# One layer of a pooling and mLSTM backbone on one core: the pooling input and its gate as seven-product pairs ahead of the attention, kept in DRAM

## The chip, the cores and the metric

The kernel runs on one core of a Trainium2 chip. The metric is device time in microseconds (us) of one execution; the time of a kernel is the median of its runs. The core has a matrix engine (TensorE, in the profile PE; its weight loads PEld), a vector engine (DVE), an activation engine (ACT), GpSimd (POOL), and a sync engine (SP) that issues most DMAs. Each engine works off its own instructions in a fixed order, and an instruction that waits holds up everything behind it on its engine.

## The reference

512 latent tokens (8 rows of 64) of width 1024 and 256 context tokens go through one layer. Cut to what the change touches:

```python
a_lat = _modulate(x, norm_mix, sh1, sc1)
p = split(a_lat @ w_in)      # pool input u, q, k, v, o, gate of pool, gate of mLSTM, 16 gate columns
...
# pooling mixer: 4 groups of 256 channels, windows 2, 4, 8, 16 on the 8 x 64 grid
mean = window_sum(window_sum(u_g, w, rows), w, cols) / count
pool_out = concat((mean - u_g) @ w_pool[g]) * scale
# mLSTM: 4 heads of 256, both directions, chunks of 128, starting from the context's state
m_out = rmsnorm(h) * gain * sigmoid(o)
y = sigmoid(p[5]) * pool_out + sigmoid(p[6]) * m_out
x = x + g1 * (y @ w_out)
x = x + g2 * swiglu(modulate(x))      # then a final rmsnorm
```

## The kernel before, in words

All operands of the big products are split into a high and a low part, and one block product is three matmuls: high by high, high by low, low by high (`mm3`, L180 to L186, so lines 184, 185 and 186 are the three matmuls of nearly every projection). Channels lie on the 128 partitions, tokens along the free dimension. `lat_tile(idx)` (L403) computes one tile of the input projection, 128 channels by 512 tokens: 24 matmuls of 512 columns, after a weight tile has come by DMA (`wr`), ACT has cast its high part (`wh`, L154) and DVE has subtracted for the low part (`wl`, L155). The 48 tiles are numbered: U0 = 0 to 7 the pool input u, Q0 8 to 15, K0 16 to 23, O0 24 to 31 (output gate), G5 32 to 39 (gate of the pool branch), G6 40 to 47 (gate of the mLSTM branch). Six of them, `FIRST`, are computed in the opening stage loop that also makes the modulated activations `aT`, in six PSUM banks.

Then come four heads. For each head h the code writes, in this order: the values; the attention, in two halves of the tokens (`scores`, then `apply`, whose matmuls are L779 to L781), with a tile of the mLSTM gates as filler between scores and apply of each half; the two pool tiles `pooled(2h)` and `pooled(2h+1)`; the transposes (`turn`, L807) of the second half; the two tanh tiles of the pool gate (G5); `pool_mix` (the product with w_pool); the gating and the sum (`finish`, L831 and L832, which sends y to DRAM, `yd`); and queries and keys of the next head. Behind each `apply`, DVE normalises the rows (L784 to L799) and takes one or two late adaLN products of 128x1024 (`late_mod`, L524).

`pooled(j)` (L438) first computes its u tile on PE with `lat_tile(U0 + j)`. Then GpSimd clears a padded buffer `pa` (L456), ACT copies u from PSUM into it (L457), DVE takes the window sums by doubling (L463 or L468 over rows, L473 over columns), multiplies with the reciprocal counts (L480), subtracts u (L481), and `tsplit` makes the high part on ACT (L173) and the low part on DVE (L174). Those two parts, `pm`, are what `pool_mix` waits for. `pa` has one buffer.

The FFN further on is computed by pairs: one gate tile and one up tile together form a 2 by 2 block of weights, and a Strassen-like scheme of seven block products replaces eight. A block product has 12 matmuls of 256 columns, so a pair takes 84 (`prepare`, `front`, `back`, `strassen`, from L997). Sums of weights are taken on DVE, the low parts of two of the blocks by a DMA of GpSimd that accumulates.

The order on PE, ACT and DVE is written out by hand inside a few stages; elsewhere the instructions are put in an order when the program is built, close to the order of the code, with later code moved forward where it is free.

Of the kernel before, what the change touches and what calls it, by code (L numbers as in the profile page):

```python
# [17 lines left out]
P = 128  # L18
# [18 lines left out]
FIRST = (24, 40, 25, 41, 8, 9)  # L37
# [12 lines left out]
def layer_kernel(ctx: ExitStack, tc, xT, cT, w0, w1, wv0, wv, wada_a, wada_b, par, crow, bg, wpool,  # L50
# [33 lines left out]
    open_pool("mix", ("m", "pm", "pa", "pb"), "right")  # L84
    open_pool("kqp", ("kq", "q"))
    open_pool("st", ("x", "cx", "ada", "row"))
# [35 lines left out]
    V.tensor_scalar(half_ps, parm[:, C_PS:C_PS + KT], 0.5, None, ALU.mult)  # L122
# [3 lines left out]
    x_sb = []  # L126
    for k in range(0, KT, 2):
        xx = tl("x", [P, 2 * T], F32, KT // 2)
        nc.sync.dma_start(xx, xT[:, k * T:(k + 2) * T])
        x_sb += [xx[:, :T], xx[:, T:]]  # L130
# [61 lines left out]

    class SumSq:
# [61 lines left out]
    rs_x = S("m")  # L255
# [44 lines left out]
    rs_c = S("m")  # L300
# [18 lines left out]
    w_first = []  # L319

# [45 lines left out]
    for k in range(KT):  # L366
# [18 lines left out]
        if k in (5, 6):  # L385
            ctx_quad(4 * (k - 5))
    manual.__exit__(None, None, None)
    wv_first += vload(wv0, DH + NG, 1)
    acc0 = dict(zip(FIRST, acc0))

# [47 lines left out]
    def pooled(j):  # L438

        w = (2, 4, 8, 16)[j // 2]  # L440
        acc = lat_tile(U0 + j)
# [11 lines left out]
        u3 = acc.rearrange("p (r c) -> p r c", r=R)  # L453
# [3 lines left out]
        nc.scalar.copy(A[:, rl:rl + R, lw:lw + W0], u3)  # L457
# [68 lines left out]

    crow_s = small([P, D], "crow_s", home="pa")
    close_pool("st")
    open_pool("att", ("vh", "vl", "Sp", "E", "gate"))
# [54 lines left out]
    def gates():  # L584
# [98 lines left out]
        yield dict(g=g, gx=gx, m0=m0, c1=c1, em=em, ws=ws, rd=rd, sa0=sa0)  # L683

# [160 lines left out]
    crow_setup()  # L845
    for h in range(H):
# [12 lines left out]
        rest = attention(h, q_, k_, v, gt, mgate((2, 3, 4, 6)[h]))  # L859
        if h == H - 1:  # L860
            close_pool("att")
            close_pool("kqp")
# [73 lines left out]

# [3 lines left out]

    def kt(q, k):
        return tuple(t[:, k * TC:(k + 1) * TC] for t in q)
# [48 lines left out]
    def ptiles(h, l, o=0):  # L994
        return [(h[:, o + i * P:o + (i + 1) * P], l[:, o + i * P:o + (i + 1) * P]) for i in range(4)]

    def prepare(j):  # L997

        a = tl("wr", [P, WMAX], F32, 3)[:, :D]
        b = tl("ur", [P, D], F32, 2)  # L1000
        nc.sync.dma_start(b, wffi[2 * j + 1])
        nc.sync.dma_start(a, wffi[2 * j])
        a11, a12, a21, a22 = a[:, :T], a[:, T:], b[:, :T], b[:, T:]
        p = {}

        def direct(nm, w, dram=None):
            h, l = S("oh", F32R), S("ol", F32R)
            nc.scalar.copy(h, w)
            if dram is None:
                V.tensor_sub(l, w, h.bitcast(F32))  # L1010
            else:
                nc.scalar.activation(l, w, AF.Copy, scale=-1.0)  # L1012
                nc.gpsimd.dma_start(l, dram, accum_op=ALU.add)  # L1013
            p[nm] = ptiles(h, l)

        def summed(names, o, h, l):
            split(sg[:, o:o + D], h, l)
            for e, nm in enumerate(names):
                p[nm] = ptiles(h, l, e * T)

        yield
        sg = tl("sg", [P, 2 * D], F32, 1, LINE)
        s1, s2, s3, s4 = (sg[:, i * T:(i + 1) * T] for i in range(4))
        direct("A11", a11)
        V.tensor_add(s1, a22, a21)
        V.tensor_add(s2, s1, a11)
        summed(("S1", "S2"), 0, wide("gh"), wide("gl"))
        yield
        direct("A12", a12, wffi[2 * j][:, T:])
        yield  # L1030
        V.tensor_add(s3, a11, a21)
        V.tensor_add(s4, s2, a12)
        yield
        summed(("S3", "S4"), D, *(tl(t, [P, WMAX], F32R, 2, LINE)[:, :D] for t in ("wh", "wl")))
        yield
        direct("A22", a22, wffi[2 * j + 1][:, T:])
        yield p

    def prepared(j):
        for p in prepare(j):  # L1040
            pass
        return p

    banks = []

    def front(j, p):

        n = j % 3
        x, w, z, y = (banks[i][:, :TC] for i in (n, 3, 4 + j % 2, 6 + j % 2))
# [317 lines left out]
```

## Time and profile before

| | |
|---|---|
| median of 3 runs | 889.85 us (888.89 to 889.96) |
| the profiled execution | 891.24 us |
| its span, first to last instruction | 889.5 us |
| outside the span | 1.74 us |
| PE busy | 877.4 us, 99% of the span |
| DVE, ACT, POOL busy | 614.8, 434.7, 66.0 us |
| bytes moved by DMA | 120.87 MB |

A matmul is put down as busy from its start to a modelled end, so rows of PE overlap, and its pace is read from start to start. In a row of the timeline the first number is the start, the second the duration, and the bracket at the end tells how long the engine was idle before it and what released it. In a row of the windows stand, after the length, busy time and count of PE, PEld, DVE, ACT and POOL, the granted TensorE clock, the DMA share and GB/s.

### The profile page before, as it was taken

Reading aid. Unit: us, or ns where it says so; the run is one execution under the profiler, and the core shown is the slowest. Engines: PE = TensorE matmul, PEld = TensorE weight load, DVE = VectorE, ACT = ScalarE, POOL = GpSimd, SP = SyncE. Lnnn points to the kernel's source line nnn. Section 1 sums busy time; section 2 is a strip of 40 time slices with the busy share of each in tenths; the row PEclk is TensorE's granted clock in tenths of the full one; section 3 lists DMA queues with packets and bytes.
Section 4 is the critical chain, followed back from the end, with each engine's and each line's share of the span. In section 5 each row is a group of like instructions: output and inputs, shape, how many; then the busy total and the mean of one; then the engine's idle time right before and its main releaser. Section 6 shows DMA issues by size and latency. Waiting matters only on the chain.

```text
span 889.5 us, 15027 instructions
## 1 busy us (share of the span) xinstructions
PE 877.4 (99%) x5913; PEld 799.9 (90%) x5913; DVE 614.8 (69%) x1187; ACT 434.7 (49%) x823; POOL 66.0 (7%) x93
## 2 busy tenths in 40 slices
PE   9999999999999999999999999999999999999996
PEld 8689798899888998889988899999889998899995
DVE  4678676868876787767886767884376753866644
ACT  3464363555345453344555446763156732656541
POOL 0000010010000100001000000110011100111000
PEclk9999999999999999999999999999999999999998
DMA  9853022435252632435343830474266643766402
GB/s 350 319 190 117 25 71 61 166 111 173 74 194 76 192 117 83 159 102 159 138 132 118 298 105 5 130 199 117 75 175 145 166 106 96 189 143 146 116 1 95
DMA packets 41445, 120.87 MB, mean 136 GB/s; under 512 B 4480, under 2 KB 8864, under 8 KB 40352
## 3 DMA queue, kind: packets, MB, share of 16 engines
q1 hardware_dynamic: 35904, 109.96, 38.2%
q0 software_dynamic: 5472, 9.96, 6.8%
q8 instruction: 46, 0.75, 0.3%
q14 instruction: 23, 0.19, 0.1%
HBM read 116.22 MB, written 3.69 MB: 135 GB/s over the span
## 4 chain that ended last, share of the span: by engine, by line
PE 91%; DVE 4%; ACT 2%; issue 2%; DMA 0%; DVEq 0%; POOLq 0%; POOL 0%; ACTq 0%
PE ps L184 20%; PE ps L186 20%; PE ps L185 20%; PE pat L334 3%; PE ps L565 3%; PE ps L566 3%; PE ps L567 3%; PE pat L781 2%; PE pat L185 2%; PE pat L184 2%; PE pat L779 2%; PE pat L186 2%; PE pat L780 2%; PE pat L140 1%; PE ps L334 1%
## 5 line engine op out<-in xcount | busy, mean ns | idle before, releaser
L184 PE MATMUL ps<-a,wh 128*128 128x512 f32 (+1 forms) x368 | 138.9, 378 | 0.0
L185 PE MATMUL ps<-a,wh 128*128 128x512 f32 (+1 forms) x368 | 138.5, 376 | 0.0
L186 PE MATMUL ps<-a,wl 128*128 128x512 f32 (+1 forms) x368 | 138.3, 376 | 0.0
L154 ACT CAST wh<-wr 128x1024 fp32r<-128x1024 f32 (+3 forms) x78 | 78.8, 1010 | 116.0 <-PE ps L185 89.3
L155 DVE TENSOR_TENSOR wl<-wr,wh 128x1024 fp32r<-128x1024 f32 (+3 forms) x78 | 91.8, 1177 | 44.3 <-ACT wh L154 43.0
L186 PEld LDWEIGHTS ps<-a,wl 128*128 128x128 f32 x368 | 69.3, 188 | 12.6
L184 PEld LDWEIGHTS ps<-a,wh 128*128 128x128 f32 x368 | 69.3, 188 | 12.2
L185 PEld LDWEIGHTS ps<-a,wh 128*128 128x128 f32 x368 | 69.3, 188 | 11.8
L186 PE MATMUL ps<-act,wl 128*128 128x512 f32 (+1 forms) x224 | 77.9, 348 | 0.7 <-DVE wl L155 0.7
L184 PE MATMUL ps<-act,wh 128*128 128x512 f32 (+1 forms) x224 | 77.8, 347 | 0.0
L185 PE MATMUL ps<-act,wh 128*128 128x512 f32 (+1 forms) x224 | 77.6, 347 | 0.0
L566 PE MATMUL ps<-wl,a 128*128 128x256 f32 (+1 forms) x192 | 54.4, 283 | 0.0
L567 PE MATMUL ps<-wh,a 128*128 128x256 f32 (+1 forms) x192 | 54.3, 283 | 0.0
L565 PE MATMUL ps<-wh,a 128*128 128x256 f32 (+1 forms) x192 | 54.3, 283 | 0.0
L1013 POOL DMA_DIRECT2D ol<-in_wffi x38 | 33.4, 887 | 255.7 <-ACT ol L1012 87.4
L184 PE MATMUL ps<-hp,gh 128*128 128x256 f32 x176 | 50.1, 285 | 1.0 <-ACT pat L1051 1.0
L1222 DVE SCALAR_TENSOR_TENSOR x<-ps,lb,x 128x512 f32<-128x512 f32 (+1 forms) x32 | 19.6, 617 | 45.2 <-PE ps L186 45.2
L184 PE MATMUL ps<-hp,oh 128*128 128x256 f32 x176 | 49.2, 280 | 0.1
L185 PE MATMUL ps<-hp,gh 128*128 128x256 f32 x176 | 49.1, 279 | 0.0
L186 PE MATMUL ps<-hp,gl 128*128 128x256 f32 x176 | 49.1, 279 | 0.0
L185 PE MATMUL ps<-hp,oh 128*128 128x256 f32 x176 | 49.0, 279 | 0.0
L186 PE MATMUL ps<-hp,ol 128*128 128x256 f32 x176 | 48.9, 278 | 0.0
(321 smaller groups left out, 2528.3 us busy)
## 6 DMA issues: line engine op xcount, KB each, us to landing
wr<-in_w SPq DMA_DIRECT2D x42, 512.0 KB, 3.5
pb<-in_wada_b SPq DMA_DIRECT2D x32, 512.0 KB, 3.6
wr<-in_wffi SPq DMA_DIRECT2D x25, 512.0 KB, 3.9
ur<-in_wffi SPq DMA_DIRECT2D x19, 512.0 KB, 4.0
ol<-in_wffi POOLq DMA_DIRECT2D x38, 256.0 KB, 5.0
ada<-in_wada_a SPq DMA_DIRECT2D x8, 1024.0 KB, 8.8
wr<-in_wffo SPq DMA_DIRECT2D x16, 448.0 KB, 3.9
wr<-in_wout SPq DMA_DIRECT2D x8, 512.0 KB, 3.7
```

The costliest lines, as they stand in the source:

```text
L154: nc.scalar.copy(wh, raw[:, :n])
L155: V.tensor_sub(wl, raw[:, :n], wh.bitcast(F32))
L184: nc.tensor.matmul(dst, wh, ah, start=first and i == 0, stop=False, skip_group_check=on)
L185: nc.tensor.matmul(dst, wh, al, start=False, stop=False, skip_group_check=on)
L186: nc.tensor.matmul(dst, wl, ah, start=False, stop=last and i == n - 1, skip_group_check=on)
L334: nc.tensor.matmul(acc0[i], w_first[k][i][w], aT[k][x], start=k + w + x == 0, stop=k == KT - 1 and w == 1)
L565: nc.tensor.matmul(acc[:, :n], ah, wh, start=kk == 0, stop=False)
L566: nc.tensor.matmul(acc[:, :n], ah, wl, start=False, stop=False)
L567: nc.tensor.matmul(acc[:, :n], al, wh, start=False, stop=kk == KT - 1)
L779: nc.tensor.matmul(o, sh_, vh[:, s, :], start=n == 0, stop=False)
L1013: nc.gpsimd.dma_start(l, dram, accum_op=ALU.add)
L1222: V.scalar_tensor_tensor(x1[j][:, c], acc[:, c], g2[:, j:j + 1], x1[j][:, c], ALU.mult, ALU.add)
```

## The change

- The 16 tiles of u and of the pool gate (U0 + j, G5 + j) are taken out of the heads. They are computed as eight pairs by the seven-product scheme, directly behind the values of head 0 and ahead of keys, queries and attention. The scheme's functions become a class `Seven` (with `prepare`, `front`, `back`, `run` unchanged in what they issue), from which the FFN's `Gated` and the new `Pool` derive.
- For the pair sums of the activations, `modulate` also writes the modulated activation in full precision over x, and DVE forms four sums and splits them into `hg` (operands N1, N2, T3, T4).
- u goes to DRAM (`ud`), the tanh of the pool gate too (`td`); the product of output gate and mLSTM gate of tiles 0 to 2 also (`gd`). They are read back by SP's DMAs in the heads. `pooled(j)` no longer has a tile product or an ACT copy: after GpSimd's clearing, a DMA brings u into `pa`.
- `FIRST` now holds the tiles 26 and 42 in place of the queries 8 and 9, which are now computed after keys(0). The attention's filler tiles start at 3 in place of 2 (`mgate(3 + h)`).
- Pools are opened in another order, `crow_setup` comes later, and two runs of 8 and 9 unused 256-column matmuls (`dense`) stand near the end.

The diff, cut to its core (`Seven` holds the former functions of the FFN):

```diff
-FIRST = (24, 40, 25, 41, 8, 9)
+FIRST = (24, 40, 25, 41, 26, 42)
...
         nc.scalar.activation(h, t1, AF.Identity, bias=shift)
+        nc.scalar.activation(src, t1, AF.Identity, bias=shift)
...
+    def sum_rest(i):
+        w11, w12, w21, w22 = quarters(i)
+        V.tensor_sub(w12, w22, w12)
+        V.scalar_tensor_tensor(w22, w11, -1.0, w22, ALU.mult, ALU.subtract)
+        V.scalar_tensor_tensor(w21, w22, -1.0, w21, ALU.mult, ALU.subtract)
...
     def pooled(j):
-        acc = lat_tile(U0 + j)
...
         nc.gpsimd.memset(A, 0.0)
-        nc.scalar.copy(A[:, rl:rl + R, lw:lw + W0], u3)
+        nc.sync.dma_start(A[:, rl:rl + R, lw:lw + W0], ud[j].rearrange("p (r c) -> p r c", r=R))
...
+    class Pool(Seven):
+        def first(self, s, z):
+            tanh_half(s[:, :TC], z)
...
+        def later(self, j, s, y, q):
+            tanh_half(s[:, TC:], y)
+            nc.sync.dma_start(td[j], s)
+
+        def done(self, j, s, x, q):
+            nc.scalar.copy(q[:, :TC], x)
+            nc.sync.dma_start(ud[j], q)
...
+    v = values(0, wv_first)
+    gen = gates()
+    next(gen)
...
+    sevens.run(0, KT)
...
     for h in range(H):
-        tg = None
         if h == 0:
-            mgate_all(0)
-            mgate_all(1)
-            q_ = queries(0)
-        v = values(h, None if h else wv_first)
-        if h == 0:
-            gen = gates()
-            next(gen)
             k_ = keys(0)
             gt = next(gen)
-            tg = [tanh_tile(G5 + e, "m") for e in range(2)]
-        rest = attention(h, q_, k_, v, gt, mgate((2, 3, 4, 6)[h]))
+            q_ = queries(0)
+        else:
+            v = values(h)
+        rest = attention(h, q_, k_, v, gt, mgate(3 + h))
...
         rest()
-        if h > 1:
-            mgate_all(2 * h + 1)
-        if tg is None and h < H - 1:
-            tg = [tanh_tile(G5 + 2 * h + e, "tmp") for e in range(2)]
+        if h == H - 1:
+            mgate_all(KT - 1)
         yb = pool_mix(h, pp)
-        if h == H - 1:
-            tg = [tanh_tile(G5 + 2 * h + e, "tmp") for e in range(2)]
+        tg = [td_tile(2 * h + e) for e in range(2)]
         for e in range(2):
+            gd_tile(2 * h + e)
             gated(yb[e], tg[e], yb[e])
...
+    dense(8)
     sd = st2.rstd_cols(HALF[1])
+    dense(9)
```

On PE, at the end of head 1's attention, this is the order before. `pat457` is the last `apply`, `ps462` and `ps475` are the two u tiles, `pat488` the transposes, `ps490` and `ps495` the two pool-gate tiles, `ps502` the first product of `pool_mix`, whose operand `pm_473` is the first pooled tile.

```order
L780 MATMUL pat457_2681<-vl_370_2084,Sp_442_2572 128x258
L781 MATMUL pat457_2681<-vh_369_2083,Sp_443_2573 128x258
L184 MATMUL ps462_2709<-a_36_226,wh_464_2712 128x512
...
L186 MATMUL ps475_2760<-a_123_599,wl_478_2764 128x512
L807 MATMUL pat488_2811<-ident_107,tmp_454_2654 128x128 [waits DVE_49,Activation_49]
L807 MATMUL pat488_2811<-ident_107,tmp_454_2654 128x128
L807 MATMUL pat488_2811<-ident_107,tmp_459_2695 128x128 [waits DVE_49]
L807 MATMUL pat488_2811<-ident_107,tmp_459_2695 128x128
L184 MATMUL ps490_2819<-a_36_226,wh_492_2822 128x512 [waits Activation_49]
...
L186 MATMUL ps495_2852<-a_123_599,wl_498_2856 128x512
L184 MATMUL ps502_2890<-pm_473_2756,wh_500_2886 128x512 [waits Activation_49]
```

Between the last `apply` and `pool_mix` stand 48 matmuls, the four transposes, and 48 matmuls more, all of 512 columns.

At the same place of the changed kernel `pat583` is the last `apply`, `pat606` the transposes, `ps610` the first product of `pool_mix` with the first pooled tile `pm_595` and its low part `pm_596`, and `ps617` the first tile of the next head's queries.

```order
L984 MATMUL pat583_3704<-vl_496_3107,Sp_568_3595 128x258
L985 MATMUL pat583_3704<-vh_495_3106,Sp_569_3596 128x258
L1011 MATMUL pat606_3772<-ident_110,tmp_580_3677 128x128 [waits DVE_49,Activation_49]
L1011 MATMUL pat606_3772<-ident_110,tmp_580_3677 128x128
L1011 MATMUL pat606_3772<-ident_110,tmp_585_3718 128x128 [waits DVE_49]
L1011 MATMUL pat606_3772<-ident_110,tmp_585_3718 128x128
L186 MATMUL ps610_3785<-pm_595_3748,wh_608_3781 128x512 [waits Activation_49]
L187 MATMUL ps610_3785<-pm_596_3749,wh_608_3781 128x512 [waits DVE_49]
L188 MATMUL ps610_3785<-pm_595_3748,wl_609_3782 128x512
...
L186 MATMUL ps617_3817<-a_38_231,wh_619_3820 128x512
```

The 96 matmuls are gone from here: the transposes follow directly on `apply`, `pool_mix` on the transposes, and the queries stand behind the first six matmuls of `pool_mix`, of which the first two wait for ACT and for DVE.

On DVE, at the end of head 1, these rows lead to the first pooled tile before: the last normalisation of the second half, the two late products (`crow_s`), and the window sums from `pa_466` to the low part `pm_474`.

```order
L799 TENSOR_SCALAR tmp_459_2695<-tmp_459_2695,rst_384_2269 128x256 [waits DVE_49]
L524 SCALAR_TENSOR_TENSOR pb_460_2703,mods_145<-pb_460_2703,crow_s_695 128x1024 [waits DMAHW1_49]
L524 SCALAR_TENSOR_TENSOR pb_461_2706,mods_145<-pb_461_2706,crow_s_695 128x1024 [waits DMAHW2_49]
L155 TENSOR_TENSOR wl_493_2823<-wr_491_2820,wh_492_2822 128x1024 [waits DMAHW7_49,PE_49,Activation_49]
L463 TENSOR_TENSOR pb_467_2743<-pa_466_2740 128x670 [waits DVE_49,Activation_49]
L463 TENSOR_TENSOR pb_468_2745<-pb_467_2743 128x536 [waits DVE_49]
L473 TENSOR_TENSOR pb_469_2747<-pb_468_2745 128x528 [waits DVE_49]
L473 TENSOR_TENSOR pb_470_2749<-pb_469_2747 128x512 [waits DVE_49]
L480 TENSOR_TENSOR tmp_472_2753<-pb_470_2749,tmp_471_2751 128x512 [waits DMAHW4_49,DVE_49]
L481 TENSOR_TENSOR tmp_472_2753<-tmp_472_2753,pa_466_2740 128x512 [waits DVE_49]
L155 TENSOR_TENSOR wl_498_2856<-wr_496_2853,wh_497_2855 128x1024 [waits DMAHW0_49,PE_49,Activation_49]
L174 TENSOR_TENSOR pm_474_2757<-tmp_472_2753,pm_473_2756 128x512 [waits Activation_49]
```

Between them stand the low parts of two weight tiles (L155).

In the changed kernel the same stretch of DVE reads so; L1003 is the former L799, L682 the former L524, L621 to L639 the window sums, L1035 the former L831.

```order
L1003 TENSOR_SCALAR tmp_585_3718<-tmp_585_3718,rst_510_3292 128x256 [waits DVE_49]
L682 SCALAR_TENSOR_TENSOR pb_586_3726,mods_148<-pb_586_3726,crow_s_2002 128x1024 [waits DMAHW1_49]
L682 SCALAR_TENSOR_TENSOR pb_587_3729,mods_148<-pb_587_3729,crow_s_2002 128x1024 [waits DMAHW2_49]
L621 TENSOR_TENSOR pb_589_3735<-pa_588_3732 128x670 [waits DVE_49]
L1035 TENSOR_TENSOR m_616_3807<-m_616_3807,m_511_3293 128x512 [waits DMAHW4_49,Activation_49]
L621 TENSOR_TENSOR pb_590_3737<-pb_589_3735 128x536 [waits DVE_49]
L1035 TENSOR_TENSOR m_374_2452<-m_374_2452,m_512_3294 128x512 [waits Activation_49]
L631 TENSOR_TENSOR pb_591_3739<-pb_590_3737 128x528 [waits DVE_49]
L631 TENSOR_TENSOR pb_592_3741<-pb_591_3739 128x512 [waits DVE_49]
L638 TENSOR_TENSOR tmp_594_3745<-pb_592_3741,tmp_593_3743 128x512 [waits DMAHW5_49,DVE_49]
L639 TENSOR_TENSOR tmp_594_3745<-tmp_594_3745,pa_588_3732 128x512 [waits DVE_49]
L176 TENSOR_TENSOR pm_596_3749<-tmp_594_3745,pm_595_3748 128x512 [waits Activation_49]
```

The sums on `pa_588` still stand behind the last normalisation and the two late products. The two weight tiles have left the stretch, and the two products of `finish` (L1035) have moved into it.

More of the change, by code (lines that the diff above doesn't have):

```diff
@@ L1080, in strassen, with first, begin, later @@
[L1080 to L1103 removed]
+    class Gated(Seven):
+        def first(self, s, z):
+            nc.scalar.activation(s[:, :TC], z, AF.Silu)
+        def begin(self, j):
+            act_tiles(j)
+        def later(self, j, s, y, q):
+            nc.scalar.activation(s[:, TC:], y, AF.Silu)
+            V.scalar_tensor_tensor(s[:, TC:], q[:, TC:], -1.0, s[:, TC:], ALU.mult, ALU.mult)
+        def done(self, j, s, x, q):
+            V.scalar_tensor_tensor(s[:, :TC], x, -1.0, s[:, :TC], ALU.mult, ALU.mult)
+            split(s, *act[j])
@@ L1209, in layer_kernel @@
     st2 = SumSq((T // 2,))
-    banks += [PS() for _ in range(4)] + [PS("pat") for _ in range(4)]
+    banks[:] = [PS() for _ in range(4)] + [PS("pat") for _ in range(4)]
     turn_ = [0]
@@ L1248, in gain, with dense @@
         nc.scalar.activation(gained[i][j][:, 0, :], x1[j][:, HALF[i]], AF.Copy, scale=pcol(C_NFIN, j))
+    def dense(n):
+        for _ in range(n):
+            nc.tensor.matmul(banks[3][:, :TC], B11[0][:, :P], B11[0][:, :TC], start=True, stop=True)
     def final(i, sd, cuts):
```

290 lines of the change are left out of this document (175 added, 115 removed).

## The prediction

> **What bounds the kernel now.** I read the page first, for the busy shares and the PE row of the slices.
>
> ```profile
> PE 877.4 (99%) x5913; PEld 799.9 (90%) x5913; DVE 614.8 (69%) x1187; ACT 434.7 (49%) x823; POOL 66.0 (7%) x93
> PE   9999999999999999999999999999999999999996
> PEclk9999999999999999999999999999999999999998
> ```
>
> PE is busy from the first slice to the last, at full clock. So the time is the sum of PE's work, and everything else is hidden as long as PE has something to do. The windows then give the pace of the two kinds of work that are exchanged, and of head 1 (from 185.60 to 288.10), whose last part begins at the end of its attention.
>
> ```profile
> 143.91:165.74 21.83, 21.83 (x99) 17.98 (x97) 16.01 (x28) 7.68 (x14) 2.21 (x6) 1.00 0.40 133
> 587.57:597.47 9.90, 9.90 (x87) 9.90 (x86) 7.42 (x13) 6.63 (x12) 1.74 (x2) 1.00 0.68 165
> 185.60:288.10 102.50, 102.45 (x633) 92.14 (x632) 76.84 (x149) 47.49 (x94) 7.21 (x11) 1.00 0.42 131
> 235.50:288.10 52.60, 52.60 (x258) 44.47 (x257) 37.97 (x59) 22.35 (x37) 4.09 (x8) 1.00 0.35 115
> ```
>
> The first row is four projection tiles in a stretch (96 matmuls of 512 columns and three that overlap), 5.46 us a tile and 0.227 us a matmul. The second is one FFN pair of 84 matmuls, 9.90 us. In the third DVE is busy 77 of 102.5 us: there is slack, but it comes from PE's having so much to do.
>
> Then I read how PE passes the end of an attention. The timeline of PE at that place of head 1:
>
> ```profile
> 235.41 0.28 PE L781 MATMUL pat<-vh,Sp 128*128 128x258 f32 x1
> 235.53 0.40 PE L184 MATMUL ps<-a,wh 128*128 128x512 f32 x1
> ```
>
> PE goes on at 235.53 without a pause, because the next thing in its order is a u tile that depends on nothing. I call 235.53 zero. The timelines of DVE, ACT and GpSimd show what has to happen after it before `pool_mix` can start:
>
> ```profile
> 236.11 0.17 DVE L786 RECIPROCAL rec<-rec 128x1 f32<-128x1 f32 x1
> 238.91 0.62 DVE L799 TENSOR_SCALAR tmp<-tmp,rst 128x256 f32<-128x256 f32 x2 [0.81 <-POOL rst L797]
> 239.44 1.22 DVE L524 SCALAR_TENSOR_TENSOR pb<-pb,crow_s 128x1024 f32<-128x1024 f32 x1
> 241.73 0.09 DVE L524 DVE_READ_ACCUMULATOR pb<-pb,crow_s 128x1 f32 x1
> 243.22 0.85 DVE L463 TENSOR_TENSOR pb<-pa 128x670 f32<-128x670 f32 x1
> 244.11 0.72 DVE L463 TENSOR_TENSOR pb<-pb 128x536 f32<-128x536 f32 x1
> 244.86 1.43 DVE L473 TENSOR_TENSOR pb<-pb 128x528 f32<-128x528 f32 x2
> 247.05 0.69 DVE L481 TENSOR_TENSOR tmp<-tmp,pa 128x512 f32<-128x512 f32 x1
> 248.80 0.69 DVE L174 TENSOR_TENSOR pm<-tmp,pm 128x512 fp32r<-128x512 f32 x1
> 250.17 0.69 DVE L831 TENSOR_TENSOR m<-m,m 128x512 f32<-128x512 f32 x1
> ...
> 247.78 0.63 ACT L173 CAST pm<-tmp 128x512 fp32r<-128x512 f32 x1
> 247.89 0.72 POOL L456 MEMSET pa<- 128x737 f32 x1 [9.02 <-ACT m L809]
> ```
>
> The rows are normalised at +4.0, the late products end at +6.3, the six steps of the window sums take 243.22 to 247.74 = 4.5, the high part comes 0.7 later. All of that is hidden today: 96 matmuls, 21.8 us, lie between `apply` and `pool_mix`.
>
> **The change part by part.**
>
> *The products.* Removed are 16 tiles of 5.46 = 87.3 us of PE; added are eight pairs of 9.90 = 79.2. The balance is **-8.1 us**. All of it counts, since PE is the bound. If the pairs are not dense, the gain goes: in the pair of the profile DVE is busy 7.42 of 9.90 us and the DMA 0.68 of its share, so I bound this between 0 and +8 for the eight (1 us a pair), and take 0.
>
> *The ends of the four heads.* The orders above show that the 96 matmuls leave just the place where they cover the chain, and nothing takes it: `apply`, transposes, `pool_mix`. DVE's rows stay behind the last normalisation and the late products, though u itself lies ready in DRAM. For head 1, from zero:
>
> - The transposes run at +4.0, for 0.3.
> - The window sums begin at +6.3 instead of +7.7 (the weight subtraction between them, 1.23, is gone). With two `finish` products among them at 0.6 each from start to start (250.17 and its kind), they end at 6.3 + 4.5 + 1.2 = 12.0. The high part is ready at 12.6, the low part at 13.2. PE has idled 12.6 - 0.3 = 12.3, and 0.4 more for the low part.
> - Six matmuls but one, then 23 of the queries, 28 x 0.227 = 6.4: PE is at 19.6. The second pooled tile needs `pa`, which has one buffer: GpSimd clears it after 12.0 (0.72, at +12.8), and SP brings u. The nearest DMA rows are those of the same size:
>
> ```profile
> tmp<-in_icnt SPq DMA_DIRECT2D x2, 256.0 KB, 3.5
> yd<-tmp SPq DMA_DIRECT2D x2, 256.0 KB, 3.6
> ```
>
> With 3.5 it lands at 16.3; 4.5 of sums and 0.63 of cast make 21.4. PE waits 1.8, and 0.4 for the low part. SP holds no weight of the next projection behind that DMA; those for queries and keys were issued ahead of it.
> - The next query tile can't have its weight buffer cast until `pool_mix` is done with it:
>
> ```profile
> L154 ACT CAST wh<-wr 128x1024 fp32r<-128x1024 f32 x60 | 62.8, 1047 | 86.5 <-PE ps L185 68.1 <-issue 7.4 <-PE pat L185 5.4
> L155 DVE TENSOR_TENSOR wl<-wr,wh 128x1024 fp32r<-128x1024 f32 x60 | 73.4, 1223 | 39.9 <-ACT wh L154 38.7
> ```
>
> that is 1.05 for the cast and most of the 1.22 for the low part, less two matmuls, 1.9.
>
> Head 1 together: 12.3 + 0.4 + 1.8 + 0.4 + 1.9 = **16.8 us**.
>
> Head 2 has the same order on PE, with a longer chain (window 8):
>
> ```profile
> 345.68 1.19 DVE L463 TENSOR_TENSOR pb<-pa 128x994 f32<-128x994 f32 x1
> ...
> 350.18 1.22 DVE L155 TENSOR_TENSOR wl<-wr,wh 128x1024 fp32r<-128x1024 f32 x1
> 351.32 0.68 DVE L473 TENSOR_TENSOR pb<-pb 128x512 f32<-128x512 f32 x1
> ...
> 353.24 0.69 DVE L481 TENSOR_TENSOR tmp<-tmp,pa 128x512 f32<-128x512 f32 x1
> ```
>
> That is 8.25, with a weight subtraction (1.14 from start to start) and a `finish` product (0.6) among it: 6.5 of its own against 4.5. The first wait is 2.0 longer; the second too, less 0.1 that two more matmuls and a longer clearing make, 1.9; and there the rest of a tile covers the weights' 1.9. Together 16.8 + 2.0 + 1.9 - 1.9 = 18.8, **19 us**.
>
> Head 0 keeps cover: the two query tiles of head 1 (`q1`) stand between its `apply` and the transposes, 48 x 0.227 = 10.9. Its window of 2 has two sums fewer (1.4), so the first tile is ready in time. Its sums end at 6.3 + 3.1 + 0.6 (the low part of a small weight) = 10.0. The second comes at 10.0 + 0.8 (clearing) + 3.5 (DMA) + 3.1 (sums) + 1.2 (`finish` products) + 0.6 (cast) = 19.2. PE is at 10.9 + 0.3 + six matmuls = 12.6: **7 us** with the low part.
>
> Head 3 has its y splits on DVE among the sums. Before, normalisation and the two pooled tiles stand like this:
>
> ```profile
> 454.71 0.61 DVE L799 TENSOR_SCALAR tmp<-tmp,rst 128x256 f32<-128x256 f32 x2 [0.81 <-POOL rst L797]
> 467.24 0.69 DVE L174 TENSOR_TENSOR pm<-tmp,pm 128x512 fp32r<-128x512 f32 x1
> 473.01 0.69 DVE L174 TENSOR_TENSOR pm<-tmp,pm 128x512 fp32r<-128x512 f32 x1 [0.69 <-ACT pm L173]
> ```
>
> The first pooled tile is complete 12.6 after the normalisation, so at about +16.6. PE has there 13 matmuls, the transposes and 35 matmuls, some 12 us. I take 1 for the transposes, 4 for the first tile, 3 for the second (it now waits for clearing and DMA, 4.2, with 5 us of cover) and 2 for the weights of w_out: **10 us**, between 3 and 15.
>
> Sum of the heads: 16.8 + 19 + 7 + 10 = **+53**. If only the first waits of heads 1 and 2 came true it would be 12.3 + 14.3 = 27.
>
> *The stage and the hand-overs.* The sums for `hg` are pushed into DVE ahead of the low weights of the values, and that subtraction is barely in time today; keys(0) needs weights whose buffers the pairs have just left; in head 0 the filler tile of the attention is spent early on by the queries. The trace of before shows none of these waits. The nearest prices are one subtraction, 1.2, for each of the first two, and between nothing and one tile, 5.46, for the third. I take 1 + 1 + 3 = **+5** (0 to 8). The x written back by ACT in the stage is one activation more there, where ACT has room (49% over the span): 0. The 17 unused matmuls near the end stand where PE is waiting for the final norm: +0.2 at most.
>
> *The clock.* Idle stretches of 12 us are new for this kernel. What it shows of them lies at its two ends:
>
> ```profile
> 0.00:4.00 4.00, 2.64 (x12) 2.64 (x13) 1.10 (x10) 1.50 (x2) 0.94 (x6) 1.00 0.38 96
> 8.00:12.00 4.00, 4.00 (x39) 4.00 (x38) 3.58 (x6) 2.17 (x4) 0.00 (x0) 1.00 1.03 410
> 884.00:886.00 2.00, 0.00 (x0) 0.00 (x0) 1.24 (x3) 0.00 (x0) 0.00 (x0) 0.61 0.53 190
> ```
>
> The granted clock falls to 0.61 within a few us of the last matmul, and the first matmuls run at 0.22 us each where 8 us later they take 0.10. By these rows a restart costs up to some 3 us (about 8 us at a mean pace near 0.6). Most of it falls into a stretch that ends with another wait of PE, where it is covered. I take +1.5 in all, 0 to 11. [...]
>
> **The sum.** Against the profiled execution: 891.2 - 8.1 + 53 + 5 + 0.2 + 1.5 = 942.8. The median of before is 1.4 lower than its profiled run, so 941.4; I say **940**.
>
> **The rivals.**
>
> 1. *The chain is not in the way, and only the products count: faster.* For it, u is ready in DRAM hundreds of us before it is used, and the window sums need nothing of `apply`. If DVE reached them before the attention's last rows, PE's wait at a head's end would be only the 3.7 to the transposes less what cover there is; with queries moved forward into it too, heads cost nearly nothing: 891.2 - 8.1 + 2 - 1.4 = 884. It decides where the head ends cost under 8 us in all, 2 a head. Against it, DVE's order has the sums behind L1003 and L682. Chance 0.10.
> 2. *The waits are there, but only the first of heads 1 and 2:* 891.2 - 8.1 + 27 - 1.4 = 909, with the hand-overs 914. For it, my second waits rest on a DMA time and on small differences. Chance 0.15.
> 3. *The clock and the pairs add:* five restarts not covered, 11, and pairs 1 us longer, 8: 940 + 17 = 957. The DMA share of 0.68 speaks for some of it; against it, the FFN's pairs with the same share run densely. Chance 0.10. [...]
> 4. *The change does not alter the time:* the gain of 8.1 equals the waits. Nothing points to just that sum. Chance 0.02.
>
> My forecast has 0.63. 0.2%, 1.8 us, is about what a measurement of this kernel can tell from no change. Faster by more than that: rival 1, 0.10. Within it: rival 4 and what lies around it, 0.03. Slower 0.87. The range runs from 908, the low end of rival 2, to 956, near rival 3; it leaves out the faster case and a little at the top.
>
> **What would show it.** In the trace after: PE idle of 12 us in head 1 and 14 in head 2 ahead of the first product of `pool_mix`, released by ACT's `pm`; two to seven us before the second pooled tile in each head, with the DMA into `pa` landing late; a pair of 9.9 us; heads 20 us shorter in PE work and only some 5 us shorter in time. The prediction is wrong if PE is dense at the head ends, if DVE's sums stand ahead of the last `apply`, or if the pairs take clearly over 10 us.

## The result and the profile after

The changed kernel takes 940.05 us (median of 4 runs, 939.0 to 940.82), the kernel before, run beside it, 889.9. The ratio is 1.0555 [1.0538, 1.0573]: 50 us slower. The profiled execution took 939.8 us, its span is 938.0, and the mean granted clock of TensorE 0.973.

The page after, busy times and two rows of the slices:

```profile
PE 887.0 (95%) x6218; PEld 813.7 (87%) x6218; DVE 652.0 (70%) x1259; ACT 468.7 (50%) x903; POOL 80.5 (9%) x109
PE   9999999999799599958999699999999999999997
PEclk9999999999899799978999899999999999999999
```

Where before every slice of PE but the last showed a 9, there are now four dents, in slices 11, 14, 18 to 19 and 23, and the clock has them at the same places. They are the ends of the four heads. PE is busy 9.6 us longer although it has less to do, mostly because matmuls at half clock (granted 0.50) take longer. The waits of PE, in total, times and longest, say for what it waits:

```profile
PE ps L186 <- ACT pm L175: 27.7, 5, 9.7
PE pat L1011 <- DVE tmp L1003: 8.2, 3, 3.7
PE ps L186 <- ACT wh L156: 2.7, 2, 1.8
PE ps L720 <- DVE wl L157: 1.2, 1, 1.2
```

`pool_mix` waits for the high part of a pooled tile, and the transposes wait for the normalised rows. Both stand right behind the attention now. The timeline of PE at the end of head 1, the place that the prediction worked through:

```profile
314.38 0.28 PE L985 MATMUL pat<-vh,Sp 128*128 128x258 f32 x1
318.37 1.09 PE L1011 MATMUL pat<-ident,tmp 128*128 128x128 f32 x4 [3.71 <-DVE tmp L1003]
326.87 0.79 PE L186 MATMUL ps<-pm,wh 128*128 128x512 f32 x1 [7.41 <-ACT pm L175]
327.60 0.79 PE L187 MATMUL ps<-pm,wh 128*128 128x512 f32 x1
...
330.74 0.40 PE L188 MATMUL ps<-a,wl 128*128 128x512 f32 x1
...
335.62 0.74 PE L186 MATMUL ps<-pm,wh 128*128 128x512 f32 x2
```

Zero, counted as in the prediction, is 314.50. The transposes run at +3.9 (predicted 4.0) and the first product of `pool_mix` at +12.4 (12.6). Here is the chain that releases it, the timeline of DVE and then GpSimd's clearing:

```profile
317.87 0.62 DVE L1003 TENSOR_SCALAR tmp<-tmp,rst 128x256 f32<-128x256 f32 x2 [0.81 <-POOL rst L1001]
318.40 1.22 DVE L682 SCALAR_TENSOR_TENSOR pb<-pb,crow_s 128x1024 f32<-128x1024 f32 x1
...
320.69 0.85 DVE L621 TENSOR_TENSOR pb<-pa 128x670 f32<-128x670 f32 x1
321.46 0.69 DVE L1035 TENSOR_TENSOR m<-m,m 128x512 f32<-128x512 f32 x1
...
326.85 0.69 DVE L176 TENSOR_TENSOR pm<-tmp,pm 128x512 fp32r<-128x512 f32 x1 [0.68 <-ACT pm L175]
330.38 0.86 DVE L621 TENSOR_TENSOR pb<-pa 128x670 f32<-128x670 f32 x1 [2.84 <-DMA pa<-ud]
...
326.29 0.71 POOL L614 MEMSET pa<- 128x737 f32 x1 [8.45 <-DVE tmp L639]
```

Normalisation, two late products, six steps of sums with two `finish` products among them, then the second pooled tile behind clearing and DMA: the rows and their order are those of the forecast. The second tile is complete at +21.1 (predicted 21.4), but PE itself comes there only at 335.62, +21.1, and so does not wait.

The stretches, first of before and then of after: the end of each head, from the end of its `apply` to the same place in the next stage.

```profile
143.91:168.95 25.04, 25.04 (x115) 20.67 (x113) 18.81 (x31) 10.13 (x18) 2.21 (x6) 1.00 0.35 116
235.53:271.43 35.90, 35.90 (x163) 29.68 (x161) 26.20 (x40) 13.55 (x22) 2.66 (x6) 1.00 0.42 139
337.98:384.75 46.77, 46.77 (x211) 38.68 (x210) 33.67 (x48) 16.60 (x26) 2.57 (x6) 1.00 0.39 124
451.32:508.99 57.67, 57.67 (x258) 47.71 (x257) 40.85 (x71) 28.17 (x45) 1.33 (x2) 1.00 0.55 179
```

```profile
81.79:160.25 78.46, 78.38 (x675) 78.18 (x674) 48.72 (x84) 46.12 (x89) 12.80 (x15) 1.00 0.74 193
226.14:247.17 21.03, 15.91 (x66) 12.45 (x65) 15.91 (x29) 6.78 (x13) 2.20 (x6) 0.88 0.44 131
314.50:343.20 28.70, 17.52 (x67) 13.02 (x65) 20.14 (x34) 7.61 (x14) 2.65 (x6) 0.76 0.36 109
409.81:442.40 32.59, 18.29 (x66) 13.48 (x65) 22.92 (x35) 7.00 (x13) 2.57 (x6) 0.74 0.26 82
509.00:558.20 49.20, 41.13 (x162) 31.96 (x161) 33.98 (x66) 20.77 (x36) 1.32 (x2) 0.90 0.51 168
```

The first row of after is the eight pairs. In the others the heads lose 48, 96, 144 and 96 matmuls of 0.2275 us (two of the counts hold one more that overlaps the edge), that is 10.9, 21.8, 32.8 and 21.8 us, but get shorter by only 4.0, 7.2, 14.2 and 8.5. The remainder is what the head ends cost. The whole account, from the places of the same instructions in the two traces:

| stretch | predicted | measured |
|---|---|---|
| eight pairs in place of 16 tiles | -8.1 | 78.46 - 16 x 5.46 = -8.9 |
| stage and hand-overs | +5 (1 + 1 + 3) | 0.4 + 1.4 + 1.3 + 0.7 = +3.8 |
| end of head 0 | 7 | 6.9 |
| end of head 1 | 16.8 | 14.6 |
| end of head 2 | 19 | 18.6 |
| end of head 3 | 10 | 13.4 |
| clock outside these; rest | +1.5; +0.2 | +0.75; -0.6 |
| sum (heads predicted as 53) | +51.6 | +48.6 |

Of the 53.5 us of the four head ends, PE idles 38.7: that is length less PE busy in the rows above. Some 12 more, an estimate from the starts of PE's timeline, are lost by matmuls, nearly all of 512 columns, that start 0.43 us apart instead of 0.2275, at a granted clock of 0.50: 1.8, 2.7, 3.4 and 4.2 us in heads 0 to 3.

### The profile page after: what moved, and what is told of

It is laid out like the page before. It is cut to its first block, busy times and chain, and to the rows that moved or that the text cites. A ratio compares the mean times of both kernels' runs of the same rounds, so it can differ in the third digit from the quotient of the medians.

```text
span 938.0 us, 15999 instructions
## 1 busy us (share of the span) xinstructions
PE 887.0 (95%) x6218; PEld 813.7 (87%) x6218; DVE 652.0 (70%) x1259; ACT 468.7 (50%) x903; POOL 80.5 (9%) x109
## 5 line engine op out<-in xcount | busy, mean ns | idle before, releaser
L157 DVE TENSOR_TENSOR wl<-wr,wh 128x1024 fp32r<-128x1024 f32 (+3 forms) x62 | 72.4, 1169 | 30.3 <-ACT wh L156 29.2
L186 PE MATMUL ps<-a,wh 128*128 128x512 f32 (+1 forms) x240 | 90.0, 375 | 0.9 <-ACT wh L156 0.9
L187 PE MATMUL ps<-a,wh 128*128 128x512 f32 (+1 forms) x240 | 89.8, 374 | 0.0
L188 PE MATMUL ps<-a,wl 128*128 128x512 f32 (+1 forms) x240 | 89.4, 372 | 0.1
L175 ACT CAST wh<-sg 128x1024 fp32r<-128x1024 f32 x27 | 28.4, 1051 | 57.7 <-PE pat L187 47.7
L176 DVE TENSOR_TENSOR wl<-sg,wh 128x1024 fp32r<-128x1024 f32 x27 | 33.1, 1225 | 33.9 <-ACT wh L175 33.8
L186 PEld LDWEIGHTS ps<-a,wh 128*128 128x128 f32 x240 | 46.2, 192 | 8.9 <-ACT wh L156 1.3
L188 PEld LDWEIGHTS ps<-a,wl 128*128 128x128 f32 x240 | 46.0, 192 | 8.2 <-DVE wl L157 0.8
L187 PEld LDWEIGHTS ps<-a,wh 128*128 128x128 f32 x240 | 46.1, 192 | 7.1
L186 PE MATMUL ps<-hp,gh 128*128 128x256 f32 x176 | 50.2, 285 | 1.0 <-ACT pat L270 1.0
L186 PEld LDWEIGHTS ps<-act,wh 128*128 128x128 f32 x224 | 42.9, 191 | 8.0 <-ACT wh L156 2.5
L186 PE MATMUL ps<-hp,oh 128*128 128x256 f32 x176 | 49.2, 279 | 0.1
```

What stands on the lines that cost most here:

```text
L157: V.tensor_sub(wl, raw[:, :n], wh.bitcast(F32))
L175: nc.scalar.copy(h, src)
L176: V.tensor_sub(l, src, h.bitcast(F32))
L186: nc.tensor.matmul(dst, wh, ah, start=first and i == 0, stop=False, skip_group_check=on)
L187: nc.tensor.matmul(dst, wh, al, start=False, stop=False, skip_group_check=on)
L188: nc.tensor.matmul(dst, wl, ah, start=False, stop=last and i == n - 1, skip_group_check=on)
```

## The experiments

My theory: PE idles at the head ends because one chain on DVE (normalisation, late products, window sums, then clearing, DMA and sums again) lost the matmuls that covered it. Rivals: the loss lies in the clock, in the pairs, or in the DMA; or each cure only moves the wait. Every kernel below is the changed kernel with the edit shown. Medians are compared with the kernel before, timed beside it on the same chip (892.05, 890.4, 891.06 and 891.07 us for the four groups), and the differences are against that. The changed kernel itself was +50.2 with the result above and +50.7 in the second group.

**The changed kernel again**, as the yardstick of its group.

> The changed kernel once more, unaltered, as the measure for the two small edits beside it: 940 to 943.

Measured: 941.08 us, 1.0574 [1.056, 1.0589], +50.7. Its trace also shows what slow matmuls cost where no wait follows. In head 3, behind PE's last wait, the same 20 matmuls take 6.42 us in the first trace and 4.68 here, because the clock was back earlier. The windows, of the first trace and then of this one:

```profile
538.64:545.06 6.42, 6.42 (x21) 5.13 (x21) 6.34 (x9) 2.37 (x4) 0.00 (x0) 0.71 0.65 201
539.17:543.85 4.68, 4.68 (x20) 3.86 (x21) 4.59 (x7) 1.22 (x2) 0.00 (x0) 1.00 0.52 150
```

This trace comes to the stretch 0.5 us later than the first, and its span ends 1.3 us earlier (936.7 against 938.0). So here, as far as two traces can show it, the clock is paid in the time.

**Are the pairs worth what they cost?** The 16 tiles are computed at the new place, but as plain tiles.

```diff
-    banks[:] = [PS() for _ in range(4)] + [PS("pat") for _ in range(4)]
-    sevens.run(0, KT)
+    for j in range(KT):
+        s, q = S("tmp"), S("tmp")
+        tanh_half(s, lat_tile(G5 + j))
+        nc.sync.dma_start(td[j], s)
+        nc.scalar.activation(q, lat_tile(U0 + j), AF.Copy, scale=-1.0)
+        nc.sync.dma_start(ud[j], q)
```

> The seven products undone, the place kept: the 16 tiles of u and pool gate are computed ahead of the attention as plain tiles of 24 matmuls of 512 columns, stored to DRAM as before (the sums of activations for the pairs are still made). Theory: pairs took 78.5 us in the trace of the changed kernel, 16 tiles take 87.3, so 940 + 9 = 949, and the head ends wait as they do. Rival (the pairs gain nothing, their work is hidden or paid elsewhere): 940.

Measured: 951.55, 1.067 [1.0643, 1.0696], +59.5. The stage of the 16 tiles in its windows:

```profile
81.71:169.48 87.77, 87.35 (x387) 71.99 (x385) 26.54 (x39) 26.75 (x38) 0.00 (x0) 1.00 0.51 166
```

It is 87.8 us against 78.5, a difference of 9.3, and the time differs by 9. The waits of the head ends stay as they were (28.8 us for `pm` and 8.1 for the transposes, against 27.7 and 8.2). So the products give their gain in full, and the loss is all elsewhere.

**Is it the clock?** Unused matmuls keep PE at work in the two waits of heads 1 and 2.

```diff
...
+        if h in (1, 2):
+            warm(28)
         rest()
+        if h in (1, 2):
+            warm(54)
```

> The clock by itself: at the ends of heads 1 and 2, 28 unused matmuls of 256 columns (3.3 us) go between the last apply and the transposes and 54 (6.3 us) between the transposes and the first product of pool_mix, that is into time in which PE waits; their results are read by nothing. Theory: the half clock behind the two long waits (9 and 13 matmuls at 0.43 instead of 0.23 us in the trace of the changed kernel, some 2 and 3 us) is hidden, since the second pooled tile is ready only when PE arrives there; the time falls by under 1 us. Rival (each restart of the clock costs what its slow matmuls lose): 5 us less, 936.

Measured: 941.28, 1.057 [1.0551, 1.0588], +50.9: no difference from the changed kernel in the same group. The windows show that the cure took:

```profile
317.00:325.00 8.00, 7.33 (x60) 6.90 (x58) 7.85 (x14) 0.84 (x2) 0.01 (x1) 1.00 0.00 0
327.00:330.00 3.00, 3.00 (x15) 2.46 (x14) 0.00 (x0) 0.00 (x0) 0.00 (x0) 1.00 0.43 93
336.00:338.00 2.00, 2.00 (x5) 1.51 (x6) 0.87 (x2) 0.00 (x0) 0.23 (x1) 0.50 1.00 371
```

The clock is 1.00 through the wait and behind it, where the changed kernel has 0.50:

```profile
328.00:330.00 2.00, 2.00 (x6) 1.52 (x6) 0.00 (x0) 0.00 (x0) 0.00 (x0) 0.50 0.58 131
```

And the timeline of PE shows where the time went instead:

```profile
334.07 0.50 PE L186 MATMUL ps<-a,wh 128*128 128x512 f32 x1 [0.91 <-ACT wh L156]
335.84 1.09 PE L186 MATMUL ps<-pm,wh 128*128 128x512 f32 x2 [1.03 <-ACT pm L175]
```

A PE that keeps its pace arrives early at the second pooled tile and at the next weights, and waits there; a new slow stretch of some 3.4 us begins at 336 (the clock is 0.51, 0.50, 0.50 and 0.78 in the four us from there, 1.00 behind them). From the end of `apply` to the keys, head 1 takes 30.28 us against 28.70 in the changed kernel, longer by about what that stretch loses (3.4 us at half the pace, 1.7), and head 2 32.07 against 32.59. In these two heads the end of the chain is what counts, and the clock is no cause of its own. Heads 0 and 3 were left as they are.

**Do the matmuls near the end matter?** `dense(8)` and `dense(9)` are left out.

> The 17 unused matmuls near the end taken out. Theory: they stand where PE waits for the final norm, so the time is the same within 0.5 us. Rival (they hold the clock up for the last columns): 1 to 2 us more without them.

Measured: 941.23, 1.0567 [1.0548, 1.0587]: the same.

**Does work of PE bring the cover back?** The queries of the next head, which stood behind the first matmuls of `pool_mix`, go ahead of the transposes in every head, as head 0 has them.

```diff
-        if h == 0:
-            q1 = queries(1)
+        if h < H - 1:
+            q1 = queries(h + 1)
         rest()
...
-            q_, k_ = queries(h + 1) if h else q1, keys(h + 1)
+            q_, k_ = q1, keys(h + 1)
```

> Cover put back, chain left as it is: in heads 1 and 2 the two query tiles of the next head (48 matmuls, 10.9 us) go between the last apply and the transposes, as head 0 has them in the changed kernel. Theory (the wait is the DVE chain behind the late products, and the second pooled tile needs the one pa buffer, a clearing and a DMA): the first wait of heads 1 and 2 shrinks from 12 and 14 us to 1 and 3, but the second tile now has no query tile in front of it, so about 7 to 9 us of wait appear there; together some 6 us less per head, 940 - 12 = 928. Rival (only missing cover counts, any 10.9 us of work there wins 10.9): 940 - 22 = 918. Rival (the waits are the clock's doing or another engine's): no change, 940.

Measured: 933.46, 1.047 [1.0446, 1.0493], +41.4. The first wait is down to 0.4 us in head 1 and 2.9 in head 2, but the timeline of PE has this at the second pooled tile of the two heads:

```profile
335.28 0.80 PE L186 MATMUL ps<-pm,wh 128*128 128x512 f32 x1 [6.56 <-ACT pm L175]
...
431.68 0.80 PE L186 MATMUL ps<-pm,wh 128*128 128x512 f32 x1 [8.98 <-ACT pm L175]
```

Cover taken from behind the first tile is missing ahead of the second. The chain on DVE ends hardly earlier (in head 1 20.6 us after the end of `apply`, 21.1 before); the gain is what the queries hide of it, 9 us and not the 12 that I expected.

**Can the sums run earlier?** Both pooled tiles are written ahead of the attention.

```diff
+        pp = [pooled(2 * h + e) for e in range(2)]
         rest = attention(h, q_, k_, v, gt, mgate(3 + h))
...
-        pp = [pooled(2 * h + e) for e in range(2)]
```

> The chain is freed, cover left as it is: the two pooled tiles of a head are written ahead of its attention, so the DVE sums no longer stand behind the last normalisation and the late products. Theory: all waits of PE on pm at the four head ends go (7, 12.5, 16, 9 us in the trace of the changed kernel), some of the 4 us wait of the transposes stays, and 12 us of DVE work that moves into each attention costs up to 5 in all: 890 to 900, 897 taken. Rival (DVE is the bound of a head, the sums only move the wait into the attention): 925 to 940.

Measured: 921.21, 1.0326 [1.0307, 1.0345], +29.2, between what the theory and its rival expected. The waits of PE:

```profile
PE pat L983 <- ACT Sp L175: 7.1, 6, 2.5
...
PE ps L186 <- ACT pm L175: 1.7, 1, 1.7
```

The wait for `pm` falls from 27.7 to 1.7 us (in the changed kernel it was 5.1, 7.4, 9.7 and 5.5 in the four heads, less than the expectation says). But now `apply` waits inside the attention for its split scores, which it did not before. The theory of the place holds, and so does half of the rival: DVE's work has to be done somewhere, and in the attention it isn't free.

**Are the late products in the way?** Those of the second half-head are written behind the pooled tiles.

```diff
...
-            late_mod(2 if h or th else 0, done)
+            if th == 0:
+                late_mod(2 if h else 0, done)
+            else:
+                ends.append(done)
...
         pp = [pooled(2 * h + e) for e in range(2)]
+        late_mod(2, ends[-1])
```

> One link of the chain taken out: the two late products behind the last normalisation (2.3 us on DVE) are put behind both pooled tiles of the head. Theory: pm comes 2.3 us earlier at each head end, both tiles, 940 - 9 = 931, a little less where the products then hold up the next weights. Rival (another link ends last: the DMA into pa, or the transposes): under 3 us, 937 or more.

Measured: 922.84, 1.0346 [1.0328, 1.0364], +30.8. The gain of 19 is twice the 2.3 us a head that two products last. The timeline of DVE, before the last normalisation, tells why:

```profile
307.99 0.70 DVE L621 TENSOR_TENSOR pb<-pb 128x536 f32<-128x536 f32 x1
308.61 0.15 DVE L990 SCALAR_TENSOR_TENSOR rec<-pat,rec 128x1 f32<-128x1 f32 x1
308.72 0.71 DVE L631 TENSOR_TENSOR pb<-pb 128x528 f32<-128x528 f32 x1
...
314.60 0.62 DVE L1004 TENSOR_SCALAR tmp<-tmp,rst 128x256 f32<-128x256 f32 x2 [0.81 <-POOL rst L1002]
```

Four of the six steps of sums now run between the small steps of the attention. The code gives the likely reason, which no run tested by itself: sums and late products take their buffers in turn from the same two, `pb`. With the products written first, the sums have to come behind them; with the products behind, the sums can be moved forward. PE's first product of `pool_mix` comes 7.2 us after the end of `apply` instead of 12.4:

```profile
315.10 0.63 PE L1015 MATMUL pat<-ident,tmp 128*128 128x128 f32 x4 [3.85 <-DVE tmp L1004]
318.27 1.22 PE L186 MATMUL ps<-pm,wh 128*128 128x512 f32 x2 [2.54 <-ACT pm L175]
```

**Do the two add?** The edits on the queries and on the late products together.

> Cover and chain together: the query tiles ahead of the transposes in heads 1 and 2, and the late products behind the pooled tiles. Theory: of what waits in the trace with the late products behind (8 us in head 1, 10 in head 2) the waits ahead of the transposes and of the first tile go, and the second tile, bound by the one pa buffer and its DMA, makes 4 and 5: 922.8 - 9 = 914. Rival (the queries' convolutions get onto DVE ahead of the sums and eat the gain): 920 or more.

Measured: 922.0, 1.0356 [1.0329, 1.0382], +31.6: the rival, they don't add. The second pooled tile of head 2, on PE:

```profile
423.81 0.80 PE L186 MATMUL ps<-pm,wh 128*128 128x512 f32 x1 [8.62 <-ACT pm L175]
```

**Is the second tile's wait the clearing and the DMA?** The same with a second buffer for `pa` (two tiles of `m` fewer make the room), so that both tiles of u can be brought ahead.

```diff
...
-        A = view(tl("pa", [P, PBW]), n, wid)
+        A = view(tl("pa", [P, PBW], F32, 2), n, wid)
```

> The kernel with cover and late products moved (922.0 us), and a second pa buffer (its room is taken from the pool of the m tiles, five in place of seven), so that the u of the second pooled tile is in place when the first is done. Theory: the waits for the second tile there (2.7, 8.8 and 2.7 us in heads 1, 2 and 3) are the clearing and the DMA in front of its sums, 4 us each; 912. Rival (DVE, which has the queries' convolutions there too, is late anyway): 918 or more.

Measured: 908.68, 1.0195 [1.0167, 1.0224], +17.6, 14 us less than without the buffer, where the theory had 10. PE's waits:

```profile
PE ps L186 <- DVE tmp L557: 7.3, 3, 5.1
PE ps L186 <- ACT pm L175: 2.1, 1, 2.1
```

Of 27.7 us for `pm`, 2.1 are left. Now a convolution on DVE (L557, the queries') comes late. This is the best complete version, and still 2% slower than the kernel before.

**Is it the amount of DVE's work?** The pooled tiles ahead of the attention, as above, and the late products taken out of the loop, with their reads.

```diff
...
-        for i in itertools.islice(late, n):
+        for i in ():
...
```

> The kernel with the pooled tiles written ahead of the attention (921.2 us), without the 32 late adaLN products: their DMAs and 37 us of DVE work are left out, and the modulation values that they make are zero. Theory (with the sums in the attention, the amount of work on DVE bounds a head: about 72 us of 81 before the change's cuts in PE work): 15 to 20 us less, 903. Rival (it is the order, single waits of the apply matmuls on their scores, and not the amount): within 4 us, 917 or more.

Measured: 894.3, 1.004 [1.0025, 1.0056], +3.2. Against the same kernel with them this is 26 us less. There they stand in the groups with this row (busy, mean ns, and the idle time ahead of them):

```profile
L682 DVE SCALAR_TENSOR_TENSOR pb<-pb,crow_s 128x1024 f32<-128x1024 f32 x32 | 38.5, 1221 | 12.0 <-DMA pb<-in_wada_b 12.0
```

38.5 us of work and 12.0 of waiting for their reads on DVE are worth some 26 on PE; whether the work, the reads or the order that they force counts more was not separated. The late products make most of what this version loses. Even without them the changed kernel does not get below the one before.

**Can the late products go where the pairs are?** They are taken out of the heads, and two stand behind each pair; in the heads the queries go first and `pa` has two buffers.

```diff
...
         def done(self, j, s, x, q):
-            nc.scalar.copy(q[:, :TC], x)
+            c = nc.scalar.copy(q[:, :TC], x)
             nc.sync.dma_start(ud[j], q)
+            late_mod(2, c)
...
-            late_mod(2 if h or th else 0, done)
...
```

> The kernel with query tiles ahead of the transposes and two pa buffers, and with 16 of the 32 late products computed during the seven-product pairs, two a pair, where DVE had 2.4 us idle of 9.9; none is left behind an apply. Theory (DVE work in the heads is what is short there, and leaving all 32 out brought 27 us, 0.84 each): the 14 that leave the attentions bring 12 of 908.7, 897; that is still behind the kernel before, whose pairs are plain tiles that cover the heads. If the pairs stay dense and the heads end without waits it could reach 888. Rival (the pairs have no room for two products, or the DMAs of the weights come late): 905 or more.

Measured: 915.46, 1.0282 [1.0267, 1.0296], +24.4: the rival. From the end of the gates to the same place in the FFN it takes 11 us less than the best version (403.6 against 414.65), but it gets to the end of the gates 15 us later (176.33 against 161.19). This is read from its fastest execution, 910.83. In the stage the products have one buffer of 512 KB, so they wait for their reads (0.71, 4.17, 3.67 and 2.04 us before the four that start between 101 and 124), and what is queued behind them on DVE waits too. First the waits of PE, then the stage's window, then a row of DVE:

```profile
PE ps L186 <- ACT pat L270: 11.4, 6, 3.7
```

```profile
81.00:172.00 91.00, 80.78 (x649) 79.59 (x648) 63.16 (x111) 46.49 (x89) 13.43 (x16) 0.94 0.83 228
```

```profile
108.88 1.23 DVE L684 SCALAR_TENSOR_TENSOR pb<-pb,crow_s 128x1024 f32<-128x1024 f32 x1 [4.17 <-DMA pb<-in_wada_b]
```

PE idles some 10 us in the 91. Whether two buffers would keep the pairs dense was not tried.

**The same with the pooled tiles ahead of the attention**, in place of the queries.

> The same 16 products during the pairs and two pa buffers, with the pooled tiles written ahead of the attention in place of the query tiles ahead of the transposes. Theory: 921 less 12 for the products and some 5 for the second buffer, 904: in the middle of an attention the sums still hold up the scores. Rival (without the products DVE has room there): 895.

Measured: 934.22, 1.0485 [1.046, 1.051], +43.2; both expectations missed. It is 14 us slower than with the late products in the heads. The stage of the pairs makes more than that: the gates begin at 178.45 against 159.90, 18.5 us later, and what follows is only some 6 us shorter, where I expected 17. The stage's window, then PE's waits:

```profile
81.00:178.45 97.45, 87.30 (x687) 85.90 (x686) 64.84 (x112) 47.47 (x90) 12.25 (x14) 0.93 0.80 216
```

```profile
PE ps L186 <- ACT pat L270: 9.2, 5, 3.6
PE pat L991 <- ACT Sp L175: 5.9, 4, 2.3
PE pat L991 <- issue: 3.7, 2, 2.6
```

The first are nearly all in the pairs. Those at `apply`, 5.9 and 3.7 us, are together no smaller than the same two were with the late products in the heads (7.1 and 2.3), which the amount of DVE's work alone does not explain; this kernel also has two buffers for `pa` and two fewer for `m`. Why the heads gain so little stays open.

## Why the prediction was right, point by point

- *The products, -8.1.* Right: -8.9. The plain tiles at the same place cost 9 us more, and a pair takes 9.81 us (78.46 / 8), so the pairs are as dense as those of the FFN.
- *The chain at the head ends.* Right in mechanism and place, and the sum agrees: 53.5 us against 53. That it agrees so closely is luck: I added up waits and weights alone, but PE idles only 38.7 us, and some 12 are matmuls at half clock, which I had put at 1.5 in another term. In head 0, 5.1 us of wait and 1.8 of slow matmuls make the 7 that I forecast as wait. For head 1, the transposes, the first product of `pool_mix` and the second pooled tile came within 0.3 us of their forecast times. Undoing its parts one by one (cover, late products, the buffer of `pa`) brought back 9, 19 (the two together no more than the second alone) and, on top of both, 14 us.
- *The second wait and the weights of heads 1 and 2, +1.8 + 0.4 + 1.9 and +3.7 + 0.4.* Here the steps are wrong, though their sum nearly holds. I let PE run at full pace from the first pooled tile on. It ran at half: from 327.60 to 330.74 seven starts take 3.14 us instead of 1.59. So it reached the second tile of head 1 just as that became ready, and the weights did not bind either. Of the waits that I expected ahead of the second tile, only those of head 0 (5.1 us) and head 3 (2.1) are there. With the clock held up, those of head 1 appear (0.91 and 1.03 us), and the time is the same. Head 1 comes out 2.2 lower than forecast: its two waits, 3.7 and 7.4 us, are 11.1 against 12.3, and the slow matmuls and small delays behind them 3.5 against 4.5.
- *Head 3, 10 (3 to 15).* Mis-sized: 13.4. PE's waits there are 0.75 for the transposes, 3.47 and 2.07 for the two pooled tiles and 1.8 for the weights, 8.1 together against my 10. Of the other 5 us, which I had not counted in this head, about 4 are slower matmuls by their starts (mean clock 0.90 over the stretch); the rest was not split further.
- *The clock, +1.5 (0 to 11).* Mis-sized, though within its bounds. The loss of matmul pace is some 13 us, 12 in the head ends and 0.75 in the keys of head 1. In heads 1 and 2 it lies where the second waits would have been, as I argued, and the run with the unused matmuls gained next to nothing there. In head 0, in those keys and behind the last wait of head 3 nothing covers it: 1.8 + 0.75 + 2.0, some 4.5 us by the starts, of which the two traces of the changed kernel show 1.7 directly. The granted clock fell to 0.50 in or just behind each long gap (waits of 5.1 us in head 0, 3.7 in heads 1 and 2, 3.5 and 2.1 in head 3). In head 1 it fell about 2.4 us behind the last matmul of `apply` (0.76 over 316 to 318, 0.50 from there), and it was back 3.9 us after the first matmul of `pool_mix` (326.87 to 330.74), in head 2 5.2 us (424.45 to 429.61). The 1.00 in the prediction's row of the first window, 0 to 4 us, is no measurement: the trace of before holds no record of the clock ahead of 7.2 us.
- *Stage and hand-overs, +5.* Measured 3.8: 0.4 at the stage's end, 1.4 at the values, 1.3 at gates and keys, and 0.7 instead of 3 in the attention of head 0.
- *The rivals.* That only the products count (884) would need the sums ahead of the attention's last rows. Moved there, they cost waits in the attention, so no version reached it. That only the first waits come true (914) fails on heads 0 and 3, which cost 20 together, and on the half clock that fills the place of the second waits. Clock and pairs together (957) are out: the plain tiles show that the pairs lose nothing, and of the 11 us for the clock some 4.5 are paid.

The forecast's sum was 3 us above the measured one, and the median of after is 0.2 us above its profiled run, where that of before was 1.4 below; so the agreement of the median to a tenth is closer than the terms are.

What stays open is which order would make the change pay. No version here beats the kernel before. The nearest complete one is 17.6 us off, and one that leaves out 32 products on DVE 3.2.

## What to carry to other kernels

Matmuls that are taken out of a stage may be the cover of another engine's chain: read from the order what then stands between the last product of the chain's start and the first that needs its end, add up the chain's rows, and only then count the saved matmuls as gain. Ask of every gap also what follows it: matmuls at half clock were free here where another wait came behind them (1.5 us in head 1), and were paid where none did (6.42 us instead of 4.68 in head 3). Moving other work into the hole uncovers the place that it came from, so shorten the chain itself first: look for what holds it back without need, a buffer shared with unrelated work or a single buffer that must be cleared and filled again. When the other engine's rows in a stage come near to PE's, earlier sums or moved products can shift the wait and not remove it, as the sums ahead of the attention and the products among the pairs did here.

## What the runs showed of the hardware

- Two short waits of PE, 0.91 and 1.03 us within 3 us, were followed by a granted clock of 0.50 (336 to 338 in the run with unused matmuls); I had looked for that only behind long gaps.
- In head 1 the 1.5 us that matmuls at half clock lost behind a gap cost nothing in the time, since a chain on another engine ended last. In head 3, with no wait behind them, 20 matmuls took 6.42 us instead of 4.68, and that was paid.
- Eight late products of 1.22 us, 9.8 together, gave back 19 us when they were written behind the sums that share two buffers with them.
